# Nine slices of layer 0 by 7 products with the table load tied, and a new head: values token-major and first, constants behind a mark

## The chip, the cores and the metric

The kernel runs on one core of a Trainium2 chip. A core has five engines that run side by side, each with its own queue of instructions: TensorE (PE in the profile; PEld is its weight load), VectorE (DVE), ScalarE (ACT), GpSimd (POOL) and SyncE (SP), which here only issues transfers. Transfers (DMA) run on 16 DMA engines; SP's go to one queue (q1), POOL's to another (q0). Matrix products are written to PSUM, eight banks of 128 x 512 floats; everything else lies in SBUF. The metric is the device time of one launch in microseconds. Before the change it is 2532.29 us, the median of three runs (2530.27 to 2533.87).

## What is computed

One inference step of a small two-layer decoder, for a prompt of 1024 tokens and 8 single-token samples that share all weights, in float32. Cut to what matters here:

```python
D_MODEL, SEQ, DEPTH, DEC_BATCH, D_FF = 1024, 1024, 2, 8, 2816     # D_FF = 22 slices of 128

def swiglu(h, w_gu, w_down):
    gate, up = jnp.split(h @ w_gu, 2, axis=-1)
    return (jax.nn.silu(gate) * up) @ w_down

for l in range(DEPTH):
    hn = rmsnorm(h, g[0])
    if l < N_A:   # layer 0: gated linear recurrence (q, f, i=v, g, q_m = hn @ w_in_a) beside memory attention
        mix, S = a_mixer(hn, w_in_a[l], lbs[l], hg_norm[l], mem_k[l], mem_v[l], w_o[l], hg_s0[l])
    else:         # layer 1: stick-breaking attention over the shared keys and values beside memory attention
        mix = b_mixer(hn, w_in_b[l - N_A], sb_bias[l - N_A], k_all, v_all, q_pos, k_pos, mem_k[l], mem_v[l], w_o[l])
    h = h + rmsnorm(mix, g[1])
    h = h + rmsnorm(swiglu(rmsnorm(h, g[2]), w_gu[l], w_down[l]), g[3])
    if l == N_A - 1:
        sb_k, sb_v = jnp.split(rmsnorm(h, g_kv) @ w_kv, 2, axis=-1)     # shared keys and values
```

## The kernel before, in words

**Tiling.** Activations lie feature-major: 128 features on the partitions, tokens along the row. The tokens are cut into two groups: group 0 is 512 prompt tokens, group 1 the other 512 and the 8 samples, 520 in all. A product in group 0 is one matmul of 512 columns, in group 1 two of 260.

**Precision.** Each float32 operand is split into a rounded high part and a rest (`fp32r` pairs). `split_w` (L253) loads four 128 x 128 blocks of a weight as one 256 KB tile (`w`, pool `wraw`, 5 buffers), ACT makes the high part (L263) and DVE the rest (L264) in a tile `ws` (pool `wspl`, 5 buffers). `proj` (L269) then does three matmuls per block: high by high, high by rest, rest by high (L277), into a PSUM pair from the pool `mmp` (two pairs, four banks). `smp` (three banks) and `nsp` (one) hold transposes, scores and sums.

**Feed-forward.** `ffn.part` (L695) goes through the 22 slices in five parts (`PARTS`, L615: 5, 5, 4, 4, 4 slices). For each slice it projects gate and up, applies Silu written as Exp, Ln, Exp (`silu`, L287) and keeps the product in a tile `m`; after the slices of a part it multiplies them by `w_down` into eight row tiles R. The last part also collects the sum of squares.

**Seven products.** For group 1 of layer 1 the class `ffn_w` (L617) does gate and up otherwise. The 520 tokens are cut in two halves of 260 and the 1024 input features in two halves of 512, so gate and up together are a 2 x 2 by 2 x 2 block product, which `gate_up_w` (L526) does with 7 block products (Strassen's scheme in Winograd's form) instead of 8. It needs four sums of the inputs, made once by `sums_w` (L329) on DVE and ACT, and four sums of weights per part, made in DRAM beforehand by `weight_sums` (L590): POOL issues eight transfers per part, four plain copies and four that add into what is there (L608, L610). Each waits for a mark, a POOL copy (L605) of one number that ACT copied (L604) from the newest result of the feed-forward, so that the transfers keep step with it. The 7 products accumulate in four banks `q0` to `q3` ("quads"), which have two buffers each; before this stage all other PSUM pools are closed (L1441). The first four slices (`plain` = 4) are done in the ordinary way with the same banks and a Silu of ACT's own table (`gate_up_q`, L501), while DVE makes the input sums. ACT keeps one set of function tables at a time; L661 asks for the set with Ln and Exp before the last down projection.

**Head.** L125 to L217: loads of the parameter rows, then of the tokens of group 0 (`xtok`), constants, masks, lower bounds, page indices. `start` (L375) scales each of four token rows by its root mean square (`rms_rows`, L365: sum of squares on ACT), transposes them on PE and splits the 8 feature tiles x. Then `mixer_a.fq` does forget gates and queries, `v` (L1015) the values: four feature-major projections, each transposed back to token-major by four transposes (`to_token`, L1005).

**Order of the work.** A planner takes instructions by their place in the program and by when they are ready, and gives each engine a fixed list; within an engine the list runs in order. `weave` (L235) interleaves several streams of work in program order by weights; `with tc.issue_after(ins)` queues the instructions of its block that are on the engine of `ins` behind `ins`. Buffers of a pool's tag are handed out in program order. The schedule is L1388 to L1445; the stages that the change touches are:

```python
    weave((chain(f1.part(2), f1.part(3), f1.part(4)), 24), (ws, 24))     # L1422, layer 0, group 1
```

Of the kernel before, what the change touches and what calls it, by code (L numbers as in the profile page):

```python
# [9 lines left out]
F32 = mybir.dt.float32  # L10
F32R = mybir.dt.float32r
# [7 lines left out]
P = 128  # L19
# [4 lines left out]
def tile_decoder(  # L24
# [22 lines left out]

    def pool(name, bufs, **kw):
        return ctx.enter_context(tc.tile_pool(name=name, bufs=bufs, **kw))
# [12 lines left out]
    cpool = pool("cpool", 4)  # L62
    banks = ctx.enter_context(ExitStack())
    mmp = banks.enter_context(tc.tile_pool(name="mmp", bufs=2, space=PSUM))
    smp = banks.enter_context(tc.tile_pool(name="smp", bufs=3, space=PSUM))
    nsp = banks.enter_context(tc.tile_pool(name="nsp", bufs=1, space=PSUM))
    single = []

    uid = [0]

    def nm(s):
        uid[0] += 1
        return f"{s}_{uid[0]}"
# [10 lines left out]
    turn = [0]  # L84

# [3 lines left out]
    def NS():  # L89
        if single:  # L90
            return S()
        return nsp.tile([P, 512], F32, tag="ns", name=nm("ns"))
# [21 lines left out]
    def S():  # L114
        if single:
            turn[0] += 1
            return Q(3 * (turn[0] % 2))
        return smp.tile([P, 512], F32, tag="s", name=nm("s"))
# [5 lines left out]
    NR = 2 * 4 * ND  # L124
    prow = tpool.tile([P, P], F32, tag="t", name="prow")  # L125
# [5 lines left out]
    xtok = [rpool.tile([P, CH, D], F32, tag="r", name="xtok0")]  # L131
    for tb in range(CH):
        nc.sync.dma_start(xtok[0][:, tb, :], x_prompt[0, tb * P : (tb + 1) * P, :])
# [7 lines left out]
    trif = const.tile([P, P], F32, name="trif")  # L141
    nc.gpsimd.affine_select(
        trif, ones, pattern=[[-1, P]], compare_op=ALU.is_ge, fill=0.0, base=0, channel_multiplier=1
    )
    trir = const.tile([P, P], F32R, name="trir")
    nc.vector.tensor_copy(trir, trif)
    cmpr = const.tile([P, P], F32R, name="cmpr")
    nc.vector.tensor_sub(cmpr, ones, trif)

    sm01 = const.tile([P, P], F32, name="sm01")  # L150
    nc.gpsimd.affine_select(
        sm01, ones, pattern=[[1, P]], compare_op=ALU.is_gt, fill=0.0, base=0, channel_multiplier=-1
    )
    sel = const.tile([P, NB, NB], F32, name="sel")
    nc.gpsimd.affine_select(
        sel, ones[:, : NB * NB].rearrange("p (b c) -> p b c", c=NB), pattern=[[1, NB], [-1, NB]],
        compare_op=ALU.is_equal, fill=0.0, base=0, channel_multiplier=0,
    )

    mask = const.tile([P, 7, 64], U8, name="mask")  # L160
    for lv in range(7):
        m = 1 << lv
        nb = 64 // m
        mf = tpool.tile([P, nb, m], F32, tag="t", name=nm("mf"))
        src = ones[:, 0:64].rearrange("p (b m) -> p b m", m=m)
        nc.gpsimd.affine_select(
            mf, src, pattern=[[-2 * m, nb], [0, m]], compare_op=ALU.is_ge, fill=0.0, base=0, channel_multiplier=1
        )
        nc.gpsimd.affine_select(
            mf, mf, pattern=[[2 * m, nb], [0, m]], compare_op=ALU.is_ge, fill=0.0, base=m - 1, channel_multiplier=-1  # L170
        )
        nc.vector.tensor_copy(mask[:, lv, :], mf.rearrange("p b m -> p (b m)"))

# [15 lines left out]
    lb = const.tile([P, H], F32, name="lb")  # L189
    oml = const.tile([P, H], F32, name="oml")  # L190
    lbt = const.tile([P, H], F32, name="lbt")
    nc.vector.tensor_sub(lbt, lbraw, lbraw)
    nc.scalar.activation(lbt, lbt, AF.Exp)
    nc.vector.reciprocal(lb, lbt)
# [1283 lines left out]
```

## Time and profile before

| | us |
|---|---|
| median of three runs | 2532.29 |
| the profiled execution | 2531.92 |
| its span (first to last instruction) | 2530.2 |
| TensorE busy | 2499.1 (99% of the span) |
| VectorE busy | 1572.9 (62%) |
| ScalarE busy | 1199.7 (47%) |
| POOL busy | 91.5 (4%) |
| weight loads q1, share of the 16 DMA engines | 39.8% |
| POOL's transfers q0, share of the 16 DMA engines | 8.9% |

Busy time adds up instructions; matmuls overlap, so a mean length of a matmul is longer than its spacing, and rates are better taken from stretches in which PE does one thing. "Idle before" is the time an engine stood still ahead of a group, with what ended it. The chain is followed back from the last instruction. Names such as L277 are lines of the kernel before.

### The profile page before, as it was taken

The numbers are of one execution on the slowest core, as the hardware profiler recorded it, in microseconds if no ns is written. First come the engines' busy times: TensorE is split into PE (matmuls) and PEld (weight loads), VectorE is DVE, ScalarE is ACT, GpSimd is POOL, SyncE is SP. The second block draws the span as 40 slices with busy tenths as digits, with TensorE's granted clock in tenths as the row PEclk, the third lists the DMA queues.
The fourth block names the chain that finished last, engine by engine and source line by source line (L and its number), as shares of the span: only waits on it lengthen the run. The fifth ranks groups of instructions, "written<-read, shape, count | busy, mean of one in ns | idle before, by whom it ended". The sixth has DMA issues, their size and how long they took to land. (4 is left out here: it accounts for less than half of the span.)

```text
span 2530.2 us, 40541 instructions
## 1 busy us (share of the span) xinstructions
PE 2499.1 (99%) x15437; PEld 2169.2 (86%) x15437; DVE 1572.9 (62%) x2811; ACT 1199.7 (47%) x2294; POOL 91.5 (4%) x139
## 2 busy tenths in 40 slices
PE   8999999999999999999999999999999999999998
PEld 6888888877877888999999989876676797999997
DVE  6666556654765576655444585667577648855665
ACT  6346543243433454555333454555454445554444
POOL 1000000000000000000111100011000000000000
PEclk9999999999999999999999999999999999999998
DMA  6352242233644446476778866444343334365542
GB/s 186 111 163 67 71 154 80 63 107 117 180 125 129 129 146 190 145 179 168 182 198 212 245 186 191 152 147 118 112 146 117 97 114 122 121 188 145 150 139 68
DMA packets 502221, 358.20 MB, mean 142 GB/s; under 512 B 19077, under 2 KB 451794, under 8 KB 502026
## 3 DMA queue, kind: packets, MB, share of 16 engines
q1 hardware_dynamic: 483466, 301.08, 39.8%
q0 software_dynamic: 18560, 54.53, 8.9%
q8 instruction: 121, 1.98, 0.3%
q14 instruction: 74, 0.61, 0.1%
HBM read 325.73 MB, written 75.94 MB: 159 GB/s over the span
## 5 line engine op out<-in xcount | busy, mean ns | idle before, releaser
L277 PE MATMUL mm<-x,ws 128*128 128x260 f32 (+1 forms) x7968 | 1421.9, 334 | 0.8 <-ACT x L401 0.8
L277 PEld LDWEIGHTS mm<-x,ws 128*128 128x128 f32 x7968 | 1191.1, 188 | 173.4 <-issue 23.5
L263 ACT CAST ws<-w 128x512 fp32r<-128x512 f32 x728 | 430.7, 592 | 747.3 <-PE mm L277 610.5
L264 DVE TENSOR_TENSOR ws<-w,ws 128x512 fp32r<-128x512 f32 x728 | 474.3, 655 | 310.7 <-ACT ws L263 294.4
L277 PE MATMUL mm<-m,ws 128*128 128x512 f32 (+1 forms) x2112 | 414.3, 347 | 0.0
L277 PEld LDWEIGHTS mm<-m,ws 128*128 128x128 f32 x2112 | 325.8, 188 | 54.6 <-issue 9.5
L669 PE MATMUL q<-m,ws 128*128 128x260 f32 x1056 | 128.8, 283 | 0.0
L669 PEld LDWEIGHTS q<-m,ws 128*128 128x128 f32 x1056 | 127.2, 188 | 0.4 <-ACT hT L487 0.2
L545 DVE TENSOR_TENSOR ws<-w,ws 128x512 fp32r<-128x512 f32 x126 | 86.5, 691 | 59.9 <-ACT ws L544 56.2
L554 PE MATMUL q<-y,ws 128*128 128x260 f32 x864 | 113.0, 283 | 0.0
L544 ACT CAST ws<-w 128x512 fp32r<-128x512 f32 x126 | 77.9, 621 | 67.7 <-PE q L669 26.9
L294 DVE TENSOR_SCALAR t<-mm 128x512 f32<-128x512 f32 (+1 forms) x82 | 56.8, 693 | 82.6 <-PE mm L277 82.3
L554 PEld LDWEIGHTS q<-y,ws 128*128 128x128 f32 x864 | 107.6, 188 | 0.0
L449 DVE TENSOR_TENSOR r<-r,mm 128x512 f32<-128x512 f32 (+1 forms) x96 | 66.1, 689 | 62.4 <-PE mm L277 61.5
L705 DVE TENSOR_TENSOR t<-t,mm 128x512 f32<-128x512 f32 (+1 forms) x66 | 45.6, 690 | 85.9 <-PE mm L277 85.9
L298 DVE TENSOR_TENSOR t<-t,t 128x512 f32<-128x512 f32 (+1 forms) x66 | 45.8, 694 | 68.1 <-ACT t L297 68.1
L554 PE MATMUL q<-x,ws 128*128 128x260 f32 x648 | 86.3, 282 | 0.0
L554 PEld LDWEIGHTS q<-x,ws 128*128 128x128 f32 x648 | 81.3, 188 | 0.0
L317 DVE TENSOR_TENSOR st<-st,n 128x512 f32<-128x512 f32 (+1 forms) x98 | 67.3, 694 | 6.6 <-ACT n L316 5.0
L285 DVE TENSOR_TENSOR m<-t,m 128x512 fp32r<-128x512 f32 (+1 forms) x88 | 61.0, 693 | 2.5 <-ACT m L284 1.4
L284 ACT CAST m<-t 128x512 fp32r<-128x512 f32 (+1 forms) x88 | 54.9, 624 | 12.7 <-DVE t L705 2.5
L1135 PEld LDWEIGHTS s<-a,a 128*128 128x128 f32 x448 | 53.4, 192 | 1.2
(334 smaller groups left out, 2466.2 us busy)
## 6 DMA issues: line engine op xcount, KB each, us to landing
w<-in_w_gu SPq DMA_DIRECT2D x334, 256.0 KB, 3.3
w<-in_w_down SPq DMA_DIRECT2D x160, 256.0 KB, 2.8
w<-in_w_in_a SPq DMA_DIRECT2D x80, 256.0 KB, 2.9
wsum<-in_w_gu POOLq DMA_DIRECT2D x18, 1024.0 KB, 9.0
w<-wsum SPq DMA_DIRECT2D x72, 256.0 KB, 3.4
w<-in_w_o SPq DMA_DIRECT2D x64, 256.0 KB, 2.9
wsum<-in_w_gu POOLq DMA_DIRECT2D x12, 1280.0 KB, 10.1
w<-in_w_mem_kv SPq DMA_DIRECT2D x32, 256.0 KB, 2.9
```

Of the source, the lines that this page charges most:

```text
L263: nc.scalar.copy(ws[:, 0, :n, :], raw[:, :n, :])
L264: nc.vector.tensor_sub(ws[:, 1, :n, :], raw[:, :n, :], ws[:, 0, :n, :].bitcast(F32))
L277: nc.tensor.matmul(ps[:, a, : PW[g]], wt, xt[k][:, xi, o : o + PW[g]], start=(k == 0 and wi == 0), stop=(k == nk - 1 and wi == 2),)
L284: nc.scalar.copy(dst[0], src)
L285: nc.vector.tensor_sub(dst[1], src, dst[0].bitcast(F32))
L294: nc.vector.tensor_scalar(sv(x, g), pv(ps, g), -44.0, None, op0=ALU.max)
L317: nc.vector.tensor_add(acc[:, :n], acc[:, :n], t[:, :n])
L449: nc.vector.tensor_add(dst, dst, pv(ps, g))
L544: nc.scalar.copy(w[:, 0, :], src)
L545: nc.vector.tensor_sub(w[:, 1, :], src, w[:, 0, :].bitcast(F32))
L554: nc.tensor.matmul(ps[:, :h], w[:, wj, k * P : (k + 1) * P], x[:, xi, :], start=(first and k == 0 and wi == 0), stop=(k == 3 and wi == 2), ...
L669: nc.tensor.matmul(pp[a][:, :h], wt, mids[k][:, xi, a * h : (a + 1) * h], start=(k == 0 and wi == 0), stop=(k == nf - 1 and wi == 2),)
```

## The change

1. **Layer 0, group 1, parts 2 to 4** are done by `ffn_w`: slices 10, 11 and 12 plainly, slices 13 to 21 by 7 products. `ffn_w` takes the layer, the first part and the row tiles that parts 0 and 1 began. Its input sums lie in tiles of the pool `apool`, some raw and split weight tiles in `bpool` and `cpool`.
2. **Weight sums for layer 0** (parts 2 to 4, 24 transfers) are woven into the first half of layer 0. The ACT copy is gone: POOL's mark reads the newest result itself, whose address is kept in `now`.
3. **Layer 1, group 1** has three plain slices instead of four; the input sums are made in 16 small steps (5, 6 and 5 per slice) behind matmuls.
4. **PSUM.** `smp` and `nsp` stay open throughout. `set_banks` closes `mmp` and opens the quads with one buffer each, or the reverse; it is called four times, the first before any work.
5. **Table load.** The request for the set with Ln and Exp is queued behind the last Silu.
6. **Head.** The token loads are issued first. Of the four sums of squares two are done by DVE. The constants, masks, bounds and indices are traced after the first x tile, their DVE work is queued behind it.
7. **Values.** For group 0 `rows_proj` makes the layer-0 values, and the shared values, token-major at once: the x blocks are the weights of the matmul and the weight rows its moving operand, so no transposes follow. In layer 0 they now come ahead of forget gates and queries.

The diff, cut to its core:

```diff
+    smp = ctx.enter_context(tc.tile_pool(name="smp", bufs=3, space=PSUM))
+    nsp = ctx.enter_context(tc.tile_pool(name="nsp", bufs=1, space=PSUM))
     banks = ctx.enter_context(ExitStack())
-    mmp = banks.enter_context(tc.tile_pool(name="mmp", bufs=2, space=PSUM))
-    smp = banks.enter_context(tc.tile_pool(name="smp", bufs=3, space=PSUM))
-    nsp = banks.enter_context(tc.tile_pool(name="nsp", bufs=1, space=PSUM))
+    def set_banks(one):
+        nonlocal mmp
+        banks.close()
+        single.clear()
+        if one:
+            single.append(banks.enter_context(tc.tile_pool(name=nm("quads"), bufs=1, space=PSUM)))
+        else:
+            mmp = banks.enter_context(tc.tile_pool(name=nm("mmp"), bufs=2, space=PSUM))
...
-    def rms_rows(xt, n):
+    def rms_rows(xt, n, dve=False):
         ss = small([P, 1], tag="rr")
+        if dve:
+            nc.vector.tensor_tensor_reduce(junk, xt, xt, 1.0, 0.0, ALU.mult, ALU.add, ss[:n])
+        else:
+            nc.scalar.activation(junk, xt, AF.Square, accum_out=ss[:n])
...
+                c = j * ND + k + 1
+                for _ in range(c * n_side // 16 - (c - 1) * n_side // 16):
+                    with tc.issue_after(ins.ins):
+                        next(side, None)
...
-                tok = small([P, 1], tag="rr")
-                nc.scalar.copy(tok, after())
-                mark = nc.gpsimd.tensor_copy(small([P, 1], tag="mk", bufs=1), tok)
+                mark = nc.gpsimd.tensor_copy(small([P, 1], tag="mk", bufs=1), now[0])
...
         def spl(self):
             self.n += 1
-            if self.pi and self.n % 8 in (1, 4, 6):
+            if (self.pi or not self.rows) and self.n % 8 in (1, 4, 6):
                 return cpool.tile([P, 2, 512], F32R, tag="c", name=nm("ws"))
...
         def raws(self):
             self.r += 1
+            if not self.rows and self.r % 2:
+                return B().rearrange("p (k m) -> p k m", k=4)
...
-                nc.scalar.preload_act_table_set("natural_log_exp_and_others")
+                with tc.issue_after(act[0].ins):
+                    nc.scalar.preload_act_table_set("natural_log_exp_and_others")
...
+    def rows_proj(W, m0, xt, dst):
+        pb = [mmp.tile([P, 2, 512], F32, tag="mm", name=nm("mm")) for _ in range(2)]
+        for k in range(ND):
+            raw = wraw.tile([P, 512], F32, tag="w", name=nm("w"))
+            nc.sync.dma_start(raw, W[k * P : (k + 1) * P, m0 : m0 + H * P])
+            ws = wspl.tile([P, 2, 512], F32R, tag="ws", name=nm("ws"))
+            nc.scalar.copy(ws[:, 0, :], raw)
+            nc.vector.tensor_sub(ws[:, 1, :], raw, ws[:, 0, :].bitcast(F32))
+            for i in range(2):
+                for wi, (xi, s) in enumerate(((0, 0), (1, 0), (0, 1))):
+                    for a in range(2):
+                        c = 2 * i + a
+                        nc.tensor.matmul(
+                            pb[i][:, a, :], xt[k][:, xi, c * P : (c + 1) * P], ws[:, s, :],
+                            start=(k == 0 and wi == 0), stop=(k == ND - 1 and wi == 2),
+                        )
+            if k % 2:
+                yield
+        nc.scalar.copy(dst[0][:, :, :512], pb[0])
+        nc.vector.tensor_copy(dst[1][:, :, :512], pb[1])
...
-    drain(start(0, x0))
+    head = start(0, x0)
+    while not made[0]:
+        next(head)
+    with tc.issue_after(made[0].ins):
...
+    drain(head)
     a0 = mixer_a(0, x0)
-    drain(a0.fq(), a0.v())
+    drain(a0.v(), a0.fq())
...
-    weave((a0.mem(), 8), (a1.fq(), 8))
+    w0 = weight_sums(0, range(2, 5))
+    weave((a0.mem(), 8), (a1.fq(), 8), (islice(w0, 6), 7))
...
-    weave((chain(f1.part(2), f1.part(3), f1.part(4)), 24), (ws, 24))
+    set_banks(True)
+    fw = ffn_w(0, o1.x, (5, 6, 5), 2, False, f1.R)
+    weave((chain(fw.part(2), fw.part(3), fw.part(4)), 24), (ws, 24))
+    f1.acc = fw.acc
+    set_banks(False)
...
-    banks.close()
-    single.append(ctx.enter_context(tc.tile_pool(name="quads", bufs=2, space=PSUM)))
-    f1 = ffn_w(1, o1.x, 4)
+    set_banks(True)
+    f1 = ffn_w(1, o1.x, (5, 6, 5), 0, True)
```

229 lines of the change are left out of this document (123 added, 106 removed).

## The prediction

> **What bounds the kernel now.** I read the page first, then the busy time by stretches of 100 us, then the chain of work that ended last, then the head, the layer-0 feed-forward stage and the start of the last stage in order of time. Busy time of the engines, and TensorE (PE) by stretch (columns: stretch, length, then busy us with instruction counts of PE, weight load, VectorE (DVE), ScalarE (ACT), POOL; clock; share of the DMA engines; GB/s):
>
> ```profile
> PE 2499.1 (99%) x15437; PEld 2169.2 (86%) x15437; DVE 1572.9 (62%) x2811; ACT 1199.7 (47%) x2294; POOL 91.5 (4%) x139
> 0.00:100.00 100.00, 90.12 (x448) 74.00 (x448) 58.82 (x114) 57.51 (x110) 7.70 (x27) 1.00 0.47 143
> 1254.00:1462.00 208.00, 208.00 (x1733) 207.71 (x1732) 105.25 (x154) 85.07 (x155) 29.44 (x45) 1.00 0.83 215
> 2500.00:2600.00 100.00, 19.50 (x143) 17.19 (x141) 13.65 (x24) 12.59 (x21) 0.00 (x0) 0.92 0.06 21
> ```
>
> PE is the bound: it lacks 31 of 2530.2 us. Some 10 are at the head, 10.7 at the tail (30.2 minus 19.5), the rest in crumbs. A matmul taken away is worth its full rate, unless it uncovers a wait. The profiled execution took 2531.92 us (span 2530.2 and 1.7 around it), 0.4 below the median of the runs, 2532.29; I sum differences and apply them to the median. A stretch of the layer-0 feed-forward, then pieces of the chain (start, length, what):
>
> ```profile
> 1300.00:1340.00 40.00, 40.00 (x336) 40.00 (x335) 18.97 (x29) 12.56 (x26) 7.77 (x12) 1.00 0.91 219
> 2206.72 1.75 PE q L1370 x16
> 2292.32 28.69 PE q L669 x240
> 2321.01 40.34 PE q L554 x336
> 2517.46 1.28 ACT L758
> 2518.75 0.26 ACT rr L758
> 2519.17 1.28 ACT L759
> ```
>
> A 260-column matmul costs 40.0/336 = 0.119 us in a plain slice and 40.34/336 = 0.120 in a 7-product slice. A 128-column transpose costs 1.75/16 = 0.109.
>
> **The change part by part.**
>
> *Ten more slices by 7 products.* A plain slice of 520 tokens is 2 x 8 x 3 x 2 = 96 matmuls of 260 columns, a 7-product slice 7 x 4 x 3 = 84. Layer 0 gains nine such slices (13 to 21), layer 1 one (3 plain instead of 4). 10 x 12 x 0.120 = **-14.4 us** of PE.
>
> A 7-product slice splits 7 weight tiles instead of 4, in 10.1 us instead of 11.5. Groups of instructions (line, engine, out<-in, shapes, count | busy us, mean ns of one | idle before, who ended it):
>
> ```profile
> L544 ACT CAST ws<-w 128x512 fp32r<-128x512 f32 x126 | 77.9, 621 | 67.7 <-PE q L669 26.9 <-PE q L554 19.7 <-DMA w<-wsum 6.8
> L545 DVE TENSOR_TENSOR ws<-w,ws 128x512 fp32r<-128x512 f32 x126 | 86.5, 691 | 59.9 <-ACT ws L544 56.2 <-DMA w<-in_w_down 2.7
> L351 DVE TENSOR_TENSOR b<-b,b 128x260 f32<-128x260 f32 x16 | 6.9, 433 | 0.0
> ```
>
> That is 7 x 0.69 = 4.8 us of DVE and 7 x 0.62 = 4.3 of ACT per slice, both under 10.1. The sums of the inputs are 16 steps of 3 DVE operations, 48 x 0.43 = 20.6 us. In layer 0 DVE was busy 105 of 208 us; nine slices add 27 x 0.69 = 18.6, the sums 20.6: 144 of 195. Covered, cost nothing; the tie of the sums' steps to a matmul names PE, and they hold no PE instruction, so they may run early. If that cover went, they would cost up to the 20.6.
>
> *Sums in layer 1.* Here DVE is full. It ends the sums just before PE needs them:
>
> ```profile
> 2147.89 2.02 PE q L512 x15
> 2180.00:2190.00 10.00, 10.00 (x86) 10.00 (x85) 10.00 (x27) 5.70 (x15) 0.00 (x0) 1.00 0.38 107
> 2189.92 0.44 DVE L285 TENSOR_TENSOR y<-b,y 128x260 fp32r<-128x260 f32 x1
> 2194.88 1.75 PE q L1370 x16
> ```
>
> The plain slices begin at 2147.9; four end at 2194.9, three would end at about 2183.5, and the first product (1.4 us) needs no sums. DVE loses one plain slice (four splits, a multiplication, a split of the result: some 4 us), so the sums end at about 2186: PE waits 0 to 5 us, I take **+1**, near the difference of those two ends.
>
> *Transposes.* Values token-major use the same number of 512-column matmuls (96) and drop 16 transposes twice (v and shared values of group 0): 32 x 0.109 = **-3.5 us** of PE. The evacuations that go lie beside PE. A value projection takes both accumulator pairs at once; the first is copied while the second still gets its last 6 matmuls, so I add nothing.
>
> *Table load.* The untied preload gave no load in the trace; the two loads stand in the chain at the end, 1.28 us each. Tied behind the last Silu, one load falls under the down projection and both leave the chain: **-2.6 us**. After it the row scalings that follow stay as they are. Layer 0 now loads Silu's set and the other one back, under PE: nothing. The Trainium skill, "ScalarE: Activation LUTs", What ACT_TABLE_LOAD costs, prices a switch of sets at about 2.66 us, the 1.283 of the load and a drain of 1.38. By that the gain would be 5.3 and the forecast 2.7 us lower. In the chain the load of 2517.46 ends at 2518.74 and the next instruction starts at 2518.75: the trace agrees with the load alone.
>
> *New head.* Rows of the head in order of time (start, length; the second row is the landing of the x loads):
>
> ```profile
> 3.03 1.30 SPq L133 DMA_DIRECT2D xtok<-in_x_prompt  x3
> DMA to landing us min/median/max: 3.8/4.8/5.8
> 10.14 1.04 ACT L368 ACTIVATE c<-xtok 128x1024 f32<-128x1024 f32 x1
> 11.87 0.75 DVE L373 TENSOR_SCALAR xtok<-xtok,rr 128x1024 f32<-128x1024 f32 x1
> 14.56 0.80 PE L277 MATMUL mm<-x,ws 128*128 128x512 f32 x1 [0.77 <-ACT x L401]
> 22.16 47.18 PE L277 MATMUL mm<-x,ws 128*128 128x512 f32 x203
> L923 DVE TENSOR_TENSOR c<-c,b 128x1024 f32<-128x1024 f32 x24 | 29.2, 1222 | 12.3 <-DMA b<-qd 12.2
> ```
>
> PE runs without holes from 22.16 on. Until then it did 17 matmuls (at 47.18/203 = 0.232) and 32 transposes, 7.4 us of work: 14.7 were lost. The four parameter loads no longer stand ahead of the last three x loads on the SP queue, so these go out 1.8 us earlier; two of the four sums of squares move to DVE (1.22 for a like operation) and no longer queue on ACT, where the last began at 10.14. Multiplications end about 1.4 us earlier (11.87 + 0.75 before). The parameter columns now arrive last, but at 0.4 us per issue still before the first x tile needs them near 11. With values first PE has 12 matmuls (2.8 us) per finished x tile instead of waiting for the next. The constants' DVE work is queued behind the first x tile; the queues of POOL and SP are not held by that. I take **-2**, between 0 and -5. Behind it a small price: the gate products used to be followed by 22 us of value matmuls, which hid the last query's activation; now the recurrence follows at once, with the memory projections beside it. Bounds 0 and 3.3 (0.69 + 3 x 0.63 + 0.69 by the rows below); **+0.5**.
>
> ```profile
> L294 DVE TENSOR_SCALAR t<-mm 128x512 f32<-128x512 f32 (+1 forms) x82 | 56.8, 693 | 82.6 <-PE mm L277 82.3
> L295 ACT ACTIVATE t<-t 128x512 f32<-128x512 f32 (+1 forms) x66 | 41.9, 635 | 14.1 <-DVE t L294 9.0
> L512 PE MATMUL q<-x,ws 128*128 128x260 f32 x384 | 46.7, 283 | 1.7 <-DVE r L449 1.7
> 2292.04 4.13 PEld L669 LDWEIGHTS q<-m,ws 128*128 128x128 f32 x34
> 2292.36 0.42 DVE L577 TENSOR_TENSOR t<-t,q 128x260 f32<-128x260 f32 x1 [0.15 <-PE q L554]
> ```
>
> *PSUM banks.* The accumulators change owner three times instead of once. The one change of before shows 1.7 us at L512; two more cost 0 to 3.4: **+2.4**. The four quads have one buffer each instead of two. After the last product DVE still reads its bank for 0.42 us (2292.36), while PE began the down projection in the other buffer at 2292.04. With one buffer PE waits up to 0.75 us, at 8 such places: 0 to 6; **+2**, since the scheduler can put the other half's matmuls first.
>
> *Weight loads against the sums in DRAM.* The stage of layer 0 that gets the 7 products also carries 24 transfers that build layer 1's weight sums:
>
> ```profile
> q0 software_dynamic: 8666, 22.83, 46.8%
> q1 hardware_dynamic: 39805, 21.61, 36.1%
> DMA to landing us min/median/max: 2.8/7.3/7.4
> DMA to landing us min/median/max: 2.7/3.7/5.4
> 1266.77 0.55 POOL L605 COPY mk<-rr 128x1 f32<-128x1 f32 x1 [23.58 <-ACT rr L604]
> 1472.76 1.01 POOL L608 DMA_DIRECT2D wsum<-in_w_gu  x1 [6.78 <-DMA wsum<-wsum]
> ```
>
> The first two rows are the queues over 1254 to 1462: q0 the sums, q1 the weight loads. The landings are those of weight tiles at 1300 to 1340, beside the sums, and at 2384 to 2424, without them. Nine slices add 27 tiles of 0.262 MB, 7.1 MB; q1 moved 21.61 MB in 0.361 x 208 = 75 us of all engines, so 24.6 us more. Demand becomes 173 + 24.6 = 198 us in a stage of 195: oversubscribed by 3. Ten raw and eight split tiles lie ahead, so bursts are bridged: 0 to 6, **+2**. The Trainium skill, "DMA: Bandwidth & Descriptors", Queues, rings and completion order, says that an engine takes the queues in turn, a packet at a time; that speaks against the change, and the 7.3 us beside 3.7 agree with it. Had the tiles shared by bytes instead, this term would be about nothing.
>
> The marks on POOL read a result itself instead of a copy by ACT. While POOL waits for a transfer (6.78 above), a tile it still has to read is held, but its next writer is a slice or a part away: nothing; without that distance, 7 us each. The 24 new transfers for layer 0 run earlier, under a full PE: nothing, or the same price per transfer.
>
> Sum: -14.4 -3.5 -2.6 -2.0 = -22.5; +1 +0.5 +2.4 +2 +2 = +7.9; together -14.6. 2532.3 - 14.6 = **2517.7 us**.
>
> **The rivals.**
>
> *Weight starvation (slower).* Place: nine layer-0 slices. A tile that lands in 7.3 us gives 36 GB/s, where a 7-product slice wants 7 x 0.262 MB in 10.1 us, 182 GB/s. If the tiles ahead run dry, each of the 24 transfers stops PE. For: the sum above exceeds the stage. Against: PE lost nothing there at a DMA share of 0.83. At 1 us each +24 in place of +2: 2539.7. From (14.6 + 2)/24 = 0.7 us per transfer on the change is slower.
>
> *Small waits eat more (faster, less).* Banks 6, owners 3.4, sums 5, recurrence 3.3 in place of 5.9: 2517.7 + 11.8 = 2529.5 at full ends, 2523.6 at half. For: PE is in order and DVE is full in layer 1. Against: the scheduler reorders matmuls.
>
> *The products bring nothing in layer 0.* If DVE's order there is bad, the slices run at a plain slice's pace: 9 x 1.44 = 13 back, 2530.7, no change. Against: 144 of 195 us busy.
>
> **How the numbers follow.** About 0.2% (5 us) can be told from no change. Forecast (2509 to 2524) 0.60; small waits (2524 to 2529) 0.18; products without gain 0.08; starvation 0.14, of it 0.12 beyond 5 us. So faster 0.80, same 0.08, slower 0.12. Low end: head -5 and no price but the two owners, 2509. High end: the last tenth cuts into starvation: 2533. The likeliest case's own range is 2509 to 2524.
>
> **What would show it.** Some 120 fewer 260-column matmuls and 32 fewer transposes; PE's busy time down by 17 to 18 us; L758 and L759 without table loads; a first matmul before 14 us and no hole after it; full 40 us of PE in every 40 of the layer-0 stage at a DMA share near 1. Wrong it would be if PE there waits for splits that wait for w, or if PE idles at each change to the down projection by more than 0.7 us.

## The result

The changed kernel takes 2539.18 us (median of five runs, 2536.31 to 2544.81) against 2532.29 (five runs beside them, 2530.27 to 2535.75): a ratio of 1.0026, 95% interval 1.0015 to 1.0037. It is slower by about a quarter of a per cent. The forecast was 2517.7, in a range of 2509 to 2533. The profiled execution took 2536.31, its span 2534.6, 4.4 more than the span before. It was the shortest of the five, so the account by stages below explains 4.4 of the 6.9 us between the medians. From here on a name such as L453 is a line of the changed kernel, or of the run that is shown.

The page of the changed kernel, its busy times, and then the busy time by stretches of 50 us in the layer-0 stage (columns as before: stretch, length, busy us with counts of PE, weight load, DVE, ACT, POOL; clock; DMA share; GB/s):

```profile
PE 2490.3 (98%) x15285; PEld 2158.8 (85%) x15285; DVE 1599.3 (63%) x2921; ACT 1204.8 (48%) x2303; POOL 116.4 (5%) x187
1254.00:1462.00 208.00, 199.45 (x1598) 197.51 (x1597) 110.71 (x208) 88.51 (x172) 36.30 (x53) 0.97 0.95 250
1250.00:1300.00 50.00, 46.88 (x370) 46.74 (x369) 24.69 (x46) 20.98 (x42) 4.12 (x6) 0.93 0.76 207
1300.00:1350.00 50.00, 46.34 (x370) 45.85 (x369) 27.33 (x53) 19.58 (x39) 7.15 (x12) 0.97 0.94 236
1350.00:1400.00 50.00, 48.03 (x393) 47.24 (x392) 27.37 (x54) 19.69 (x39) 7.46 (x13) 1.00 1.06 267
1400.00:1450.00 50.00, 50.00 (x417) 49.86 (x416) 28.35 (x52) 25.60 (x50) 16.16 (x20) 1.00 1.01 281
1450.00:1500.00 50.00, 46.19 (x225) 37.82 (x223) 35.42 (x60) 25.57 (x45) 3.26 (x6) 0.97 0.89 242
```

There are 152 matmuls fewer, the 120 and 32 foretold. PE's busy time fell by 8.8 us, half of the 17 to 18 foretold, and the stage that was full before (208.00 of 208) now has 199.45, with the DMA engines at 0.95 where they stood at 0.83. The granted clock falls below 1 in three of the four stretches in which PE was not busy throughout.

To see where the time went I matched the instructions that both traces hold (same line of code, same tiles) and took how much later each starts. The differences between the checkpoints, in us:

| part | forecast | measured |
|---|---|---|
| head, values first, recurrence behind the queries (to 500 us) | -2 -1.75 +0.5 = -3.25 | -2.0 |
| 24 transfers for layer 0 (issued from 232 to 625 us), and on to 945 | 0 | +0.6 |
| shared values token-major, and up to the stage (to 1230) | -1.75 | -2.1 |
| layer-0 stage (1230 to 1470) | -13.0 for nine slices, +2 for the DMA, +2.4 for owners, a part of the +2 for banks | **+8.9** |
| layer 1's group 0 (to 1990) | 0 | -2.4 |
| start of layer 1's group 1 (to 2240) | -1.44 +1, and banks | +3.6 |
| its products (to 2505) | banks | +0.3 |
| tail | -2.6 | -2.5 |

Two rows are wrong by much: the layer-0 stage by 16 to 20 us, and the start of layer 1 by some 4. The -2.4 in layer 1's group 0 was not foretold, and nothing here tells what it comes from.

**Inside the layer-0 stage.** PE's rows there (start, length, instructions; in brackets the idle time before and what ended it). L453 are the plain slices, L622 the down projections, 192 matmuls for each of three parts; L631 is DVE's evacuation of a down projection's bank, L390 the same in the ordinary parts:

```profile
1253.29 37.27 PE L453 MATMUL q<-x,ws 128*128 128x260 f32 x288 [3.12 <-DVE r L390]
1300.49 11.85 PE L622 MATMUL q<-m,ws 128*128 128x260 f32 x96
1316.01 13.52 PE L622 MATMUL q<-m,ws 128*128 128x260 f32 x96 [3.66 <-DVE r L631]
...
1369.75 9.01 PE L622 MATMUL q<-m,ws 128*128 128x260 f32 x72
1379.17 6.23 PE L622 MATMUL q<-m,ws 128*128 128x260 f32 x48 [0.40 <-DVE r L631]
1386.97 9.02 PE L622 MATMUL q<-m,ws 128*128 128x260 f32 x72 [1.57 <-DVE r L631]
1436.19 14.72 PE L622 MATMUL q<-m,ws 128*128 128x260 f32 x120
1453.13 4.79 PE L622 MATMUL q<-m,ws 128*128 128x260 f32 x24 [2.22 <-DVE r L631]
1458.62 6.14 PE L622 MATMUL q<-m,ws 128*128 128x260 f32 x48 [0.69 <-DVE r L631]
```

The 7-product slices between them have no hole. The down projections do, and each hole names DVE's evacuation (L631). What DVE was waiting for stands in the order of time around the first of them (L484 loads a weight tile of a 7-product slice; L489 and L490 split it on ACT and DVE, as L204 and L205 split the others):

```profile
1302.11 3.42 SPq L484 DMA_DIRECT2D w<-wsum  x2
1306.67 0.62 ACT L204 CAST ws<-w 128x512 fp32r<-128x512 f32 x1 [2.26 <-PE q L622]
1307.64 0.65 POOL L556 DMA_DIRECT2D wsum<-wsum  x1 [0.32 <-issue]
1314.28 0.62 ACT L489 CAST ws<-w 128x512 fp32r<-128x512 f32 x1 [6.98 <-DMA w<-wsum]
1314.93 0.69 DVE L490 TENSOR_TENSOR ws<-w,ws 128x512 fp32r<-128x512 f32 x1 [6.91 <-ACT ws L489]
1315.54 0.76 DVE L631 TENSOR_TENSOR r<-r,q 128x260 f32<-128x260 f32 x2
```

This is the chain of one hole. SP asks for two weight tiles of the next part's first slice from 1302.11 on. At 1307.64 POOL starts an adding transfer. ACT's next instruction splits one of those tiles and stands 6.98 us for it; DVE's next is the rest of that split and stands 6.91 us for ACT; the evacuation of a finished bank is behind it in DVE's list, and PE has no free bank until it is done. PE did not need the late tile yet: the weights of its next products had been split before. It needed a bank, and the engine that empties banks stood at the late tile.

After the longer waits PE runs slowly for a while: 96 matmuls take 13.52 us behind the wait of 3.66, and 11.85 when nothing is ahead; 24 take 4.79 behind 2.22, where 24 x 0.120 is 2.9. The granted clock is 0.50 from 1317.1 to 1320.4 and from 1453.6 to 1457.0.

**The start of layer 1.** PE's waits between 2120 and 2230 us (waiting line and what it waited for: us, times, longest):

```profile
PE q L453 <- DVE r L390: 1.5, 1, 1.5
PE q L453 <- DVE ws L205: 1.0, 2, 0.8
PE q L499 <- DVE t L517: 0.7, 1, 0.7
PE q L499 <- ACT q L506: 0.2, 1, 0.2
PE s L1365 <- DVE r L377: 0.2, 1, 0.2
```

Before, only one wait stood here, at the same place (1.7 us). DVE is busy for 9.3 to 10 of every 10 us from 2150 to 2190, and with three plain slices its sums, the splits for the plain slices and those for the first products all come due earlier.

**The tail.** ACT in the last microseconds:

```profile
2522.19 0.73 ACT L636 ACTIVATE r<-r,par 128x520 f32<-128x520 f32 x1
2524.16 0.26 ACT L713 ACTIVATE rr<-ns,epsb 128x4 f32<-128x4 f32 x1 [1.24 <-PE ns L711]
```

No table load stands between them, and the tail is 2.5 us shorter, about what two loads of 1.28 make.

### The profile page after: what moved, and what is told of

Same layout as the page of the kernel before. It is cut to its first block, busy times and chain, and to the rows that moved or that the text cites. A ratio compares the mean times of both kernels' runs of the same rounds, so it can differ in the third digit from the quotient of the medians.

```text
span 2534.6 us, 40515 instructions
## 1 busy us (share of the span) xinstructions
PE 2490.3 (98%) x15285; PEld 2158.8 (85%) x15285; DVE 1599.3 (63%) x2921; ACT 1204.8 (48%) x2303; POOL 116.4 (5%) x187
## 5 line engine op out<-in xcount | busy, mean ns | idle before, releaser
L218 PE MATMUL mm<-x,ws 128*128 128x512 f32 (+1 forms) x6624 | 1235.6, 342 | 1.1 <-DVE r L631 0.9
L218 PEld LDWEIGHTS mm<-x,ws 128*128 128x128 f32 x6624 | 1017.5, 188 | 166.4 <-issue 23.9
L204 ACT CAST ws<-w 128x512 fp32r<-128x512 f32 (+1 forms) x672 | 395.6, 589 | 633.6 <-PE mm L218 480.0
L205 DVE TENSOR_TENSOR ws<-w,ws 128x512 fp32r<-128x512 f32 (+1 forms) x672 | 434.9, 651 | 287.7 <-ACT ws L204 281.2
L622 PE MATMUL q<-m,ws 128*128 128x260 f32 x1632 | 204.9, 286 | 8.5 <-DVE r L631 8.5
L622 PEld LDWEIGHTS q<-m,ws 128*128 128x128 f32 x1632 | 200.2, 191 | 11.1 <-DVE r L631 4.6
L490 DVE TENSOR_TENSOR ws<-w,ws 128x512 fp32r<-128x512 f32 x164 | 112.5, 691 | 85.7 <-ACT ws L489 83.7
L489 ACT CAST ws<-w 128x512 fp32r<-128x512 f32 x164 | 101.4, 621 | 108.6 <-PE q L622 36.4
L499 PE MATMUL q<-x,ws 128*128 128x260 f32 x1008 | 134.5, 283 | 0.0
L499 PEld LDWEIGHTS q<-x,ws 128*128 128x128 f32 x1008 | 126.5, 188 | 0.2 <-DVE ws L490 0.2
L499 PE MATMUL q<-y,ws 128*128 128x260 f32 x912 | 119.6, 284 | 0.9 <-DVE t L517 0.7
L499 PEld LDWEIGHTS q<-y,ws 128*128 128x128 f32 x912 | 113.6, 189 | 1.5 <-DVE t L517 0.9
L453 PE MATMUL q<-x,ws 128*128 128x260 f32 x576 | 73.9, 290 | 5.7 <-DVE r L390 4.7
L453 PEld LDWEIGHTS q<-x,ws 128*128 128x128 f32 x576 | 72.1, 195 | 7.6 <-ACT a L225 3.3
L390 DVE TENSOR_TENSOR r<-r,mm 128x512 f32<-128x512 f32 (+1 forms) x72 | 49.3, 685 | 32.6 <-PE mm L218 31.7
L631 DVE TENSOR_TENSOR r<-r,q 128x260 f32<-128x260 f32 x112 | 42.5, 421 | 41.6 <-PE q L622 41.6
```

What stands on the lines that cost most here:

```text
L204: nc.scalar.copy(ws[:, 0, :n, :], raw[:, :n, :])
L205: nc.vector.tensor_sub(ws[:, 1, :n, :], raw[:, :n, :], ws[:, 0, :n, :].bitcast(F32))
L218: nc.tensor.matmul(ps[:, a, : PW[g]], wt, xt[k][:, xi, o : o + PW[g]], start=(k == 0 and wi == 0), stop=(k == nk - 1 and wi == 2),)
L390: nc.vector.tensor_add(dst, dst, pv(ps, g))
L453: ins = nc.tensor.matmul(pp[a][:, :h], wt, xt[k][:, xi, a * h : (a + 1) * h], start=(k == 0 and wi == 0), stop=(k == ND - 1 and wi == 2),)
L489: nc.scalar.copy(w[:, 0, :], src)
```

## The experiments

Theory: in the layer-0 stage the weight loads starve beside the 24 transfers of layer 1's weight sums, and the in-order engines hand the wait on. Rivals: the quads' single buffers; the change of owner at the entry with the input sums ahead of the evacuation; another part of the change. Each kernel ran beside the kernel before, on the same chip; ratios are to that, with 95% intervals. Shifts are of matched instructions in the profiled runs.

**1. Layer 0 by plain slices, the rest as changed.**

```diff
-    set_banks(True)
-    fw = ffn_w(0, o1.x, (5, 6, 5), 2, False, f1.R)
-    weave((chain(fw.part(2), fw.part(3), fw.part(4)), 24), (ws, 24))
-    f1.acc = fw.acc
-    set_banks(False)
+    weave((chain(f1.part(2), f1.part(3), f1.part(4)), 24), (ws, 24))
```

The transfers of `w0` go too.

> Layer 0 is done by plain slices in the old banks, its own 24 transfers are gone, all else is as in the changed kernel. If the loss is in layer 0 alone: 2527 to 2530, below the kernel before by the head, the values and the table load (-1.9, -1.5, -2.9) less the slow start of layer 1 (+3.6). If the other parts are what makes the kernel slower: 2535 to 2540.

Measured: 2527.96, ratio 0.9984 (0.9975 to 0.9993). The stage is full again, as its row shows. Head and tail bring what they brought (-2.5 and -2.9 in this profile); the shared values bring 0.7. So layer 0's products, with all that belongs to them, cost some 11 us (2539.2 to 2528.0), and the rest of the change is a gain. The busy times of this run over the stage (columns as above):

```profile
1230.00:1470.00 240.00, 240.00 (x1959) 237.22 (x1958) 117.92 (x177) 91.94 (x150) 36.95 (x53) 1.00 0.85 220
```

**2. The 24 transfers out of the stage, earlier.**

```diff
-    weave((chain(a1.merge(), a1.mem()), 12), (a1.mem_sample(), 20), (chain(f0.part(2), f0.part(3)), 16))
-    drain(f0.part(4))
+    ws = weight_sums(1, range(5))
+    weave((chain(a1.merge(), a1.mem()), 12), (a1.mem_sample(), 20), (chain(f0.part(2), f0.part(3)), 16), (islice(ws, 18), 16))
+    weave((f0.part(4), 8), (islice(ws, 6), 6))
...
-    weave((chain(fw.part(2), fw.part(3), fw.part(4)), 24), (ws, 24))
+    drain(fw.part(2), fw.part(3), fw.part(4))
```

> The 24 transfers that build layer 1's weight sums are taken out of the layer-0 stage and issued some 250 to 550 us earlier. Starvation (mine): in the layer-0 stage TensorE lost 9.4 us in waits inside and behind the down projections and some 3.4 us to half clock behind them; these go, the entry wait (3.1 us and half clock) stays: 2525 to 2529 against 2539.2, DMA share of the stage from 0.95 to below 0.6. One buffer per PSUM bank, or the owner change, as the cause: nothing comes back, 2537 to 2541. A third way: the transfers cost the same where they go, 2535 to 2539.

Measured: 2530.91, ratio 0.9995 (0.9986 to 1.0004): 8.3 us come back, fewer than expected of starvation and more than expected of the third way. The rows of PE in the stage:

```profile
1261.66 34.67 PE L453 MATMUL q<-x,ws 128*128 128x260 f32 x288 [1.99 <-DVE r L390]
1306.26 23.36 PE L622 MATMUL q<-m,ws 128*128 128x260 f32 x192
1369.84 23.36 PE L622 MATMUL q<-m,ws 128*128 128x260 f32 x192
1433.41 23.35 PE L622 MATMUL q<-m,ws 128*128 128x260 f32 x192
```

Each down projection is whole, in 23.36 us. In the changed kernel the three took 29.0 (1300.49 to 1316.01 + 13.52), 26.2 and 28.6, which is 13.8 more; the plain slices took 37.27 instead of 34.67, 2.6 more, behind a wait longer by 1.1. Together 17.5, and the matched instructions say 17.6: the stage's loss against this run is accounted for, and it goes with the transfers. Against the kernel before the stage is now ahead by 8.8 us.

But 8.5 us were paid where the transfers went, between 690 and 900 us. Without them the DMA engines stood at 0.29 to 0.47 there; with them they are as full as in the layer-0 stage for half of the time (two rows of this run):

```profile
700.00:750.00 50.00, 48.41 (x208) 36.08 (x207) 30.87 (x52) 16.29 (x36) 6.06 (x10) 1.00 1.00 267
850.00:900.00 50.00, 48.78 (x250) 40.67 (x249) 27.61 (x43) 22.18 (x37) 5.58 (x8) 1.00 1.02 255
```

DVE and PE of this run at 800 us:

```profile
797.04 1.23 DVE L890 TENSOR_TENSOR c<-c,ss 128x1024 f32<-128x1024 f32 x1 [5.61 <-DMA c<-in_cache_mem_v]
799.98 0.68 DVE L390 TENSOR_TENSOR r<-r,mm 128x512 f32<-128x512 f32 x1
800.72 1.65 PE L218 MATMUL mm<-m,ws 128*128 128x512 f32 x6 [2.59 <-DVE r L390]
```

The same chain with another tile: DVE stands at a late load of the samples' memory, an evacuation is queued behind it, PE waits 2.59 us for the bank.

**3. The input sums of layer 0 behind the last evacuation.**

```diff
-                    with tc.issue_after(ins.ins):
+                    with tc.issue_after((tie or ins).ins):     # tie: the last L390 of the part before
                         next(side, None)
```

> The input sums of layer 0 are queued on VectorE behind the last evacuation of the part before, instead of running ahead of it. If the sums ahead of that evacuation make the entry wait (mine): the 3.1 us wait shrinks below 1 us and the half clock behind it goes, 2533 to 2536. If the change of owner costs that by itself: no difference, 2538 to 2540. If the sums then come too late for the first product of layer 0: a wait of up to 8 us there, 2540 to 2545.

Measured: 2536.93, ratio 1.0016 (1.0007 to 1.0025), some 2 us better than the changed kernel, though the intervals overlap. The entry wait stayed, with another cause. ACT, DVE and PE at the entry in order of time:

```profile
1249.89 0.62 ACT L204 CAST ws<-w 128x512 fp32r<-128x512 f32 x1 [3.90 <-DMA w<-in_w_gu]
1250.54 1.53 DVE L205 TENSOR_TENSOR ws<-w,ws 128x512 fp32r<-128x512 f32 x2 [3.21 <-ACT ws L204]
1251.99 0.69 DVE L390 TENSOR_TENSOR r<-r,mm 128x520 f32<-128x520 f32 x1
1252.82 37.26 PE L453 MATMUL q<-x,ws 128*128 128x260 f32 x288 [3.19 <-DVE r L390]
```

With the sums gone, a split of a late tile stands ahead of the evacuation. The owner change makes PE wait for that evacuation, and whatever is ahead of it sets the price.

**4. Two buffers for each quad,** the pools of transposes and scores closed meanwhile, as before.

```diff
-            single.append(banks.enter_context(tc.tile_pool(name=nm("quads"), bufs=1, space=PSUM)))
+            single.append(banks.enter_context(tc.tile_pool(name=nm("quads"), bufs=2, space=PSUM)))
         else:
             mmp = banks.enter_context(tc.tile_pool(name=nm("mmp"), bufs=2, space=PSUM))
+            smp = banks.enter_context(tc.tile_pool(name=nm("smp"), bufs=3, space=PSUM))
+            nsp = banks.enter_context(tc.tile_pool(name=nm("nsp"), bufs=1, space=PSUM))
```

> The four quads have two buffers each again, the pools of transposes and scores being closed while they are open. If one buffer per quad is the cause: 2530 to 2535. By the starvation theory the late weight stays late: within 1.5 us of the changed kernel, 2537.5 to 2540.5.

Measured: 2538.94, ratio 1.0017 (1.0008 to 1.0026). The rival falls: PE waits 13.3 us in the stage, where it waited 12.5 with single buffers, only at other places (`PE mm <- DVE r` 5.7, at the entry 4.6). And in experiment 2 the down projections have single buffers and no hole.

**5. The transfers later.** They are woven into the stage of layer 1's group 0 (1650 to 2050 us).

```diff
+        (chain(f0.part(0), f0.part(1), f0.part(2), f0.part(3)), 34), (ws, 24),
```

> The 24 transfers leave the layer-0 stage to the other side: they are woven into the stage of layer 1's group 0, some 300 to 800 us later. The layer-0 stage should come out as when they were issued early, 17 us ahead of the changed kernel; if transfers cost 0.4 us each wherever they stand (9.6 us when early), 2530 to 2532; if only in stages with other large loads, 2521 to 2526; if POOL's gathers come late behind the marks, above 2535.

Measured: 2552.40, ratio 1.0073 (1.0059 to 1.0086). The layer-0 stage gave back 13 us, and 36 were lost behind it in the profiled execution, the longest of five (2563.01). PE waited there for the scores, 10.8 and 7.3 us at L1302 (2.8 and 1.8 in the changed kernel) and 6.2 at L1314, while POOL stood at marks (97.7 and 88.1 us) ahead of its gathers of cached keys and values. That the gathers came late behind the marks is read from these rows, not tried by itself.

**6. Smaller packets.** If the packets take turns one for one, adds in pieces of 512 B should leave the loads a larger share. The adds of both layers are cut, and in a second kernel the plain copies as well (`max_dma_last_dim=w` for `4 * w`):

```diff
                     if add:
-                        nc.gpsimd.dma_start(d, a, accum_op=ALU.add)
+                        for r in (0, 256):
+                            nc.gpsimd.dma_start(d[r : r + 256], a[r : r + 256], accum_op=ALU.add, max_dma_last_dim=w)
```

> The adding transfers of the weight sums move rows in pieces of 512 B (640 B in the first parts) instead of 2 KB (2.5 KB), each as two transfers of half the rows; nothing else changes. If the weight loads starve because their 512 B packets take turns with 2 KB packets one for one (mine): a tile beside an add lands in 4 to 5 us instead of 7.3, the waits at the down projections of layer 0 fall below 4 us in all, 2529 to 2534 against 2539.2. If what counts is the load of the DMA engines as a whole: no gain, and more packets to move, 2538 to 2546.

> As the run with short adds, and the plain copies in pieces of 512 B and 640 B too. If copies starve the loads as adds do: a little better again than short adds, by 1 to 3 us. If only adds do: the same within 1 us. If the load of the engines counts: slower than short adds by 2 or more.

Measured: 2560.81, ratio 1.0112 (1.0095 to 1.0129), and with short copies too 2600.42, ratio 1.0264 (1.025 to 1.0278). Only "slower than short adds by 2 or more" fits, by 40 us: the load of the engines counts. With short adds the first hole of the stage went, one of 5.9 us came between 1350 and 1400, and up to 1465 the stage was ahead of the changed kernel by 7 us; then 30 and 65 us were lost behind it. DVE's waits there in the run with short adds, and the queues over 1254 to 1462 (packets, MB, share of 16 engines), q0 first of the changed kernel, then of the run with all short:

```profile
DVE r L371 <- POOL mk L551: 29.4, 3, 17.7
```

```profile
q0 software_dynamic: 9223, 24.76, 48.5%
```

```profile
q0 software_dynamic: 18030, 16.29, 44.3%
```

One MB of sums took 2.0% of the engines' time in this stretch with long packets and 2.7% with short ones, beside the weight loads. The sums ran past the end of the stage, POOL's marks were late, and the residual had to wait for marks that still had to read its row tiles.

To take that hold away, ScalarE copies the number for the mark, as in the kernel before:

```diff
-                mark = nc.gpsimd.tensor_copy(small([P, 1], tag="mk", bufs=1), now[0])
+                tok = small([P, 1], tag="rr")
+                nc.scalar.copy(tok, now[0])
+                mark = nc.gpsimd.tensor_copy(small([P, 1], tag="mk", bufs=1), tok)
```

> Short adds as before, and POOL's marks read a number that ScalarE copied out of the newest result, as in the kernel before, so that a late mark holds no row tile. Mine: in the run with short adds the layer-0 stage gained some 8 us and 30 us were lost behind it because the residual (VectorE, L371) waited for marks that were late; without that hold 2530 to 2535. If the 30 us come from the transfers themselves crowding the loads of the next stage: above 2550 still.

Measured: 2557.57, ratio 1.0099 (1.0084 to 1.0114), as long as the second guess said. But in its profile the loss is now inside the layer-0 stage, 13 us, and not behind it. The hold moved: the copy waits for POOL to free the small tile, and ACT's list stands behind it (a row of ACT in this run).

```profile
1472.23 0.19 ACT L552 COPY rr<-r 128x1 f32<-128x1 f32 x1 [16.33 <-POOL mk L553]
```

Short adds with the early place of experiment 2:

> The 24 transfers of layer 1 early and the adds short. Issued early with 2 KB packets they cost 9.6 us where they went (690 to 900 us). If that price too is starvation by packets: it falls to 0 to 3 us, 2521 to 2525 against 2530.9. If the price is the load of the engines: 9.6 us or more, 2530 to 2536.

> As the run before it, with four plain slices in layer 1: 0 to 2 us below it.

Measured: 2541.20, ratio 1.0032 (1.0020 to 1.0043), and 2541.24, ratio 1.0033 (1.0020 to 1.0045). The price at 690 to 950 us rose from 8.6 to some 19 us and, with four plain slices, 23; the DMA share is 0.99 at 690 to 800. So shorter packets did not pay for the longer time that the sums take from the engines. The share of the turn-taking in the starvation stays open: it was not tried apart from the load.

**7. Four plain slices in layer 1,** layer 0 plain.

```diff
-    f1 = ffn_w(1, o1.x, (5, 6, 5), 0, True)
+    f1 = ffn_w(1, o1.x, (4, 4, 4, 4), 0, True)
```

> Layer 0 plain as before, and in layer 1 four plain slices ahead of the products instead of three, the sums' 16 steps spread over four. With three the start of layer 1 came out 2.4 us worse than with four in the kernel before, where the plain slice less was to bring 1.4. If the sums come late with three (mine): 2524 to 2527 against 2528.0. If the finer steps or the single buffers make the start slow: 2528.5 to 2530, the slice alone.

Measured: 2526.94, ratio 0.9973 (0.9963 to 0.9983). The slice more costs 1.44 us of PE, and between 2100 and 2240 us the kernel loses 1.0 against the one before, where with three plain slices it loses 2.2; the waits at L499 and L205 are gone. The intervals of this pair overlap (0.9963 to 0.9983, and 0.9975 to 0.9993 with three), and in the two early kernels of experiment 6 the same step brought nothing (2541.20 and 2541.24). So the tenth 7-product slice gained nothing that could be measured; that it loses is likely, and not shown.

**8. Other places for layer 1's transfers,** all with four plain slices. First 14 at 690 to 900 us and 26 at 1000 to 1236, where the changed kernel has 16; the lines that differ from experiment 2:

```diff
-    weave((chain(a1.merge(), a1.mem()), 12), (a1.mem_sample(), 20), (chain(f0.part(2), f0.part(3)), 16), (islice(ws, 18), 16))
-    weave((f0.part(4), 8), (islice(ws, 6), 6))
+    weave((chain(a1.merge(), a1.mem()), 12), (a1.mem_sample(), 20), (chain(f0.part(2), f0.part(3)), 16), (islice(ws, 11), 16))
+    weave((f0.part(4), 8), (islice(ws, 3), 6))
...
-    weave((chain(b0.sb(), b0.mem()), 30), (chain(f1.part(0), f1.part(1)), 18), (islice(ws, 16), 17))
+    weave((chain(b0.sb(), b0.mem()), 30), (chain(f1.part(0), f1.part(1)), 18), (ws, 26))
```

> 2 KB packets as they were, four plain slices in layer 1, and the 40 transfers of layer 1 spread thinner: 14 instead of 24 at 690 to 900 us, 26 instead of 16 at 1000 to 1236 us, none in the layer-0 stage. If a transfer costs 0.4 us wherever it stands: 2529 to 2532. If it costs only where one meets the next (three at once stood in the queue at 830 us): 2521 to 2526.

Measured: 2532.57, ratio 1.0001 (0.9992 to 1.0009). The ten more at 1000 to 1236 us cost 0.4 us, the 14 about 8, as much as 24 cost at the same place in experiment 2: the price does not go by the count. In this run and the four that follow the last two of the 26 are issued 3 to 13 us after the layer-0 stage has begun, so that its entry is not free of them. Then the 14 at 880 to 1000 us, without and with the tie of experiment 3:

```diff
+    weave((f0.part(4), 8), (islice(ws, 6), 6))
+    weave((f0.finish(True), 9), (o1.mm(a1.xo, 1, 5), 4), (islice(ws, 4), 4))
+    weave((b0.heads(), 8), (o1.finish(), 17), (islice(ws, 4), 6))
```

> Layer 1's 40 transfers avoid the layer-0 stage and the memory stage (690 to 880 us): 14 between 880 and 1000 us, 26 between 1000 and 1236 us, where 26 cost nothing in the run before; four plain slices in layer 1. If the nine slices cost time only through starved loads (mine): the 17 us that the layer-0 stage got back when nothing ran beside it stay, without the 8 to 10 us paid in the memory stage: 2521 to 2526, below the 2526.9 of plain layer 0. If a transfer has a price of 0.4 us anywhere: 2527 to 2531.

> The same with the input sums of layer 0 behind the last evacuation. In the run with that tie alone the entry wait stayed, as a late weight tile stood ahead of the evacuation in its place. With no transfer beside it no tile is late there: the entry wait of 2.0 us goes below 1, and the time falls by 1 to 2 us. If the change of owner has a price of its own: no difference, within 0.7 us.

Measured: 2550.47, ratio 1.0066 (1.0052 to 1.0079), and 2543.31, ratio 1.0040 (1.0027 to 1.0054). Those 14 cost 25 us, most of it in two holes, of which this is the first (ACT, DVE and PE without the tie):

```profile
919.93 0.62 ACT L204 CAST ws<-w 128x512 fp32r<-128x512 f32 x1 [8.15 <-DMA w<-in_w_o]
923.71 0.63 ACT L257 ACTIVATE n<-m 128x520 f32<-128x520 f32 x1
924.45 1.29 DVE L258 TENSOR_TENSOR st<-st,n 128x520 f32<-128x520 f32 x2
925.80 2.07 PE L247 MATMUL ns<-st,ones 128*128 128x512 f32 x2 [11.51 <-DVE st L258]
```

ACT stands 8.15 us at a late tile with the last squares of a norm behind it, and PE can do nothing until the norm is reduced. The tie makes the layer-0 stage 5 us better here. Little of that is the entry wait (1.59 us without the tie, 1.42 with it). Most is a second wait, of the third plain slice for the Silu of the second, which the tie removes:

```profile
PE q L453 <- ACT t L464: 2.9, 1, 2.9
```

Without the tie ACT stood 9.89 us ahead of that Silu, at the split of a late tile of a 7-product slice (L489, 1305.24); with it that split stands behind the Silu in ACT's list. It is the same chain a third time. At last the 14 beside layer 0's 24, at 480 to 690 us, with and without the tie:

```diff
-    weave((a0.mem(), 8), (a1.fq(), 8), (islice(w0, 6), 7))
+    weave((a0.mem(), 8), (a1.fq(), 8), (islice(w0, 10), 11))
...
-    weave((a1.core(), 22), (f0.part(0), 9), (islice(w0, 8), 9))
+    weave((a1.core(), 22), (f0.part(0), 9), (chain(islice(w0, 6), islice(ws, 6)), 13))
...
-    weave((a1.sample(), 6), (a1.gate(), 4), (f0.part(1), 9), (w0, 5))
+    weave((a1.sample(), 6), (a1.gate(), 4), (f0.part(1), 9), (islice(ws, 8), 9))
```

> Layer 1's 40 transfers stand 14 with those of layer 0 at 480 to 690 us (38 in all there) and 26 at 1000 to 1236 us; none at 690 to 1000 us nor in the layer-0 stage; four plain slices in layer 1, the input sums of layer 0 behind the last evacuation. In the two runs before it the layer-0 stage gave back 13 us without and 18 us with that tie, but ScalarE stood at late tiles at 911 and 1017 us ahead of a reduction of the norm (9.6 to 11.5 us of TensorE each). If the price is paid only where such a reduction or a tight load stands behind a late tile (mine): 2520 to 2525. If 38 transfers at 480 to 690 us meet such a place too: 2528 to 2540.

> The same without the tie of the sums: 3 to 5 us more than with it, if the tie's gain of the two runs before holds.

Measured: 2528.19, ratio 0.9975 (0.9965 to 0.9985), and 2530.55, ratio 0.9991 (0.9983 to 1.0000). The layer-0 stage is 9.2 and 5.0 us ahead of the kernel before, and the 38 transfers (issued from 300 us on) cost 12.5 and 8 us at 550 to 690. (With the tie the profiled execution is the longest of eight, 2532.38.) The version with the tie beats both kernels, and is no better than plain layer 0 with four plain slices (0.9973). In no arrangement tried did the nine slices pay for their weight sums.

## Why the prediction was wrong

**The failed step** is "Weight loads against the sums in DRAM": "Ten raw and eight split tiles lie ahead, so bursts are bridged: 0 to 6, +2". The demand was about right: q1 took 49.7% of 208 us, 103 us, when the sums were out of the way (99.6 foretold), and the sums 48.5%, 101 (97 in the row before). The row of q1 in experiment 2:

```profile
q1 hardware_dynamic: 57025, 30.16, 49.7%
```

The price was not. It measured 17.6 us (experiment 2), on average 0.73 us for each of the 24 transfers, three times the upper bound. Two things were missing. The tiles ahead bridge a late tile only if the engines that split it may go on with other work; ACT and DVE run their lists in order, and DVE's holds the evacuations that free PE's banks. So a late tile stops PE before PE needs it. And after such a stop PE runs slowly, which the sum did not count. "Full 40 us of PE in every 40 of the layer-0 stage at a DMA share near 1" is what the trace refutes.

The rival "weight starvation" had the place, the cause and nearly the price: 1 us for each transfer in the forecast, 0.73 on the chip. It had a chance of 0.14. That its 2539.7 met the 2539.18 so closely is luck: at 0.73 its sum comes to 2533.3, and the rest is what the start of layer 1, the head and the nine slices fell short of. It also said "if the tiles ahead run dry"; the trace shows PE stopping before that. What was set against it, that PE lost nothing at a DMA share of 0.83, says little: where the 24 transfers went in experiment 2, PE lost 3.5 us between 750 and 800 at a share of 0.74. The Trainium skill, "DMA: Bandwidth & Descriptors", Queues, rings and completion order, on engines that take queues in turn, pointed the same way; the runs agree that loads starve beside the sums, and experiment 6 does not show that the turn by packets is why.

**Ten more slices, -14.4.** Right for layer 0 as far as the matmuls go, and 4 us short in time: with nothing beside it the stage is 8.8 us ahead in experiment 2, of 13.0, and 2.8 of the rest are the entry and the end of the stage (1.99 and 0.83 us). In the other runs that moved the transfers it is 9.2 and 9.3 ahead with the tie, and 4.3 to 5.0 without it. Layer 1's tenth gained nothing that could be measured.

**Sums in layer 1, +1.** Mis-sized: between 2120 and 2240 us -0.4 was due and +3.3 came. In the profiles of experiment 7 the fourth plain slice, less its own work, takes some 2.6 us back (2.2 - 1.0 + 1.44); other profiles have 2.0 to 4.8 us lost here with three slices and 1.0 to 3.2 with four, so part of it is scatter.

**"The sums' steps are covered; if that cover went, up to 20.6."** They ran early, as foretold, and ahead of the last evacuation. Cover was lost at two points, the entry and the third plain slice: the tie gives back 4.2 and 5.0 us in experiment 8, most of it at the second.

**PSUM banks, +2.4 and +2.** Two buffers gave nothing that can be told from none (1.0017 against 1.0026, intervals overlapping), and single ones show no hole in experiment 2: the +2 was none. The owner change costs what stands ahead of the evacuation, 1.4 to 4.2 us at each entry with single buffers.

**Transposes, -3.5; table load, -2.6; head, -2.** About right: -2.0 for the shared values; -2.5 at the tail, which is the load of 1.28 twice, and not the 5.3 that the Trainium skill, "ScalarE: Activation LUTs", What ACT_TABLE_LOAD costs, would give with its drain; and -2.0 at the head with the first values, from -1.0 to -2.9 in other profiled runs, of -3.25. The first value matmul starts at 15.27 us, not before 14.

**The 24 transfers for layer 0, "nothing".** Right within 0.6 us as they stood (up to 945 us), but by little room: with 14 more beside them the 38 cost 8 to 12.5.

## What to carry to other kernels

A transfer that builds something to save matmuls was paid here nearly wherever it was put, and the price was set by what stands behind the late tile on the in-order engines (an evacuation, the reduction of a norm), not by whether the tile is needed yet: before counting such a transfer as covered, read what is queued behind the instruction that takes each load. Where demand on the DMA engines comes near the length of the stage, take the oversubscribed case as the forecast and not as its edge; and try the rest of a change without its most hungry part, which here was the gain.

## What the hardware showed that was not expected

Some short waits of PE are followed by slow matmuls. In the changed kernel 288 matmuls took 37.27 us behind a wait of 3.12, and 34.67 in experiment 2 behind 1.99; 24 took 4.79 behind 2.22, and 24 x 0.120 is 2.9; 72 took 9.02 behind 1.57, near the 8.6 of full rate. The granted clock reads 0.50 for 6.83 us at the first of these waits and for 3.41 us at the third, and 1.00 at the two that cost nothing more. So a wait of 2.2 us cost some 4. In all 18 profiles together, between the head and the tail, no wait of PE under 1.8 us comes with such a half-clock stretch and each of 2.83 or more does; between the two some do and some do not (2.46 at 1717 us of the changed kernel does not). The Trainium skill, "TensorE: Matmul & The Clock Gate", HAM oscillation — how this bites in real kernels, sets the limit for idle gaps at about 3.4 us; here one of 2.22 was enough, and one of 1.83 in experiment 4.

The sums in pieces of 512 B (640 B in the first parts) took a third more of the engines' time for each MB (2.7% against 2.0% of the stretch).

Not settled: why ten more transfers at 1000 to 1236 us cost 0.4 to 1.9 us (five runs of experiment 8), where 14 cost 8 to 25 in three other places.
